# Seven-product pairs in five blocks of the up projections of a GLA and MoBA decoder trunk

## The chip, the cores and the metric

One core of one Trainium2 chip. The time is device microseconds of one execution of the whole program; lower is better. Engines: TensorE (PE; its weight loads are PEld), VectorE (DVE), ScalarE (ACT), GpSimd (POOL) and SyncE (SP, which issues the weight transfers).

## The reference

A trunk of two layers on 256 tokens with model width 2048, all in float32. Layer 0 mixes tokens with gated linear attention (GLA), layer 1 with block attention (MoBA) on a shared K and V. After each comes a gated feed-forward block, which is where most of the change lies:

```python
def conv_ffn(x, norm_w, w_up, conv_w, conv_b, w_down):
    h = rms_norm(x, norm_w) @ w_up            # 2048 x 11264
    hp = jnp.pad(h, ((0, 0), (CONV_WIDTH - 1, 0), (0, 0)))
    acc = conv_b
    for j in range(CONV_WIDTH):
        acc = acc + conv_w[j] * hp[:, j:j + S]
    a, u = jnp.split(acc, 2, axis=-1)
    return (jax.nn.silu(a) * u) @ w_down      # 5632 x 2048
```

## The kernel before

Every large matrix product is made in float32 precision from a reduced-precision matmul format: each operand is split into a high and a low part, and three products (high by high, low by high, high by low) are added in PSUM. One matmul takes 128 rows of depth, 128 tokens and 512 weight columns. Operands of the activations are made once per norm; the weights are streamed.

**The weight stream** (class WeightStream, lines 62 to 166) loads chunks of 128 x 2048 through SP into three raw buffers and splits each 1024-column half: ScalarE casts the high part `whi` (line 151), VectorE subtracts it to get `wlo` (line 153). The half's parts come from pools of three buffers each. Halves are split in a fixed order, up to two steps ahead of TensorE in the program (three in blocks with seven-product pairs). One call of step() hands one half to TensorE; jobs that were put off with after(n, job) run n steps later.

**Plain groups** (gemm_tok, line 296): 512 output columns, 8 steps of 12 matmuls, 96 in all, into two PSUM banks. High parts are line 305, the low part of the weights line 308. Each up projection has 22 such groups J.

**Blocks of pairs** (down, line 334, matmuls at line 361): 1024 output columns at once. The depth is taken in pairs k of 256 rows, so that a pair is a product of 2 x 2 matrices of blocks (two depths, two halves of the columns, two halves of the tokens). A plain pair makes the eight block products with 24 matmuls in two steps. A pair marked + in ORDERS makes seven block products of sums and differences instead, by Strassen's and Winograd's scheme: 21 matmuls in four steps. It needs sums of the weights (t13 and t24, lines 112 to 114: one VectorE operation of 1024 columns, two of 512), four halves to split instead of two (one of 512 columns, three of 1024), and sums of the activations (combine, line 314). The pairs after the bar in an order, the tail, come last and finish first the left column half (f = 0), then the right (f = 1), two steps each for two tail pairs. The seven sums p1 to p7 and p8 lie in eight PSUM banks; for names in DIRECT they are put together by one ScalarE copy and eight VectorE additions of 512 columns (lines 413 to 428). Before the change the K, MoBA query, gate, output and down projections use blocks of this kind; the up projections use only plain groups.

**After an up group**: ScalarE scales its two banks into `tok` (line 792), VectorE transposes (line 793), POOL stores the tile in DRAM (line 797) and loads it back feature-major (line 803). 7 and 9 steps after the group's end two convolutions run (convolve, line 807): two ScalarE activations (line 812), four VectorE operations of some 255 columns (lines 816, 818), a Silu, a product (line 821) and a split into the pair `hid`, VectorE's part of which is line 438. Seven of the hidden pairs (EARLY) are also combined there for the down projection.

**Memory**: a pool of 38 shared slots of 128 x 512 words or less holds operands, sums, `hid`, the weight sums and some of the split buffers; six temporary buffers hold short-lived tiles.

**Gates and start**: gated (line 745, its activations at line 627) makes the operands of the GLA output projection from transfers that POOL issues (line 527); for the last two gate heads it runs 12 and 13 steps after the head's product. At the start eight idle products of zeros keep TensorE occupied (line 223) while ScalarE's queue loads the input (line 229); the first operand `xw` is made at line 268.

Of the kernel before, what the change touches and what calls it, by code (L numbers as in the profile page):

```python
# [37 lines left out]
def _order(text):  # L38
# [13 lines left out]
    "k": [_order("0 1+ 2 3+ 4+ | 5 6 7")],  # L52
    "mq": [_order("0 1 2+ 3 4 | 5 6 7")],
    "g": [_order("0 2 5 1+ 3+ 4+ | 6 7")],
}
DIRECT = ("k", "mq", "g")

# [4 lines left out]
class WeightStream:  # L62
# [4 lines left out]
    def __init__(self, tc, raw, parts):  # L67
        self.tc, self.nc, self.raw, self.parts = tc, tc.nc, raw, parts
        self.chunks, self.halves = [], []
        self.tiles, self.split = {}, {}  # L70
        self.n_dma = self.n_split = 0
        self.cuts, self.lead, self.deep, self.free = {}, {}, set(), set()
        self.sums, self.slot, self.first = {}, None, None
        self.latest = []
# [53 lines left out]
    def prefetch(self, i):  # L128
        nc = self.nc
        while self.n_split < len(self.halves):  # L130
# [17 lines left out]
            for a, b in ((0, 512), (512, 1024)) if n < 2 else ((0, src.shape[1]),):  # L148
                with self.tc.issue_after(self.first) if n + a else nullcontext():
                    with self.in_order(n, 0):  # L150
                        one = nc.scalar.copy(hi[:, a:b], src[:, a:b])  # L151
                with self.in_order(n, 1):
                    two = nc.vector.tensor_sub(lo[:, a:b], src[:, a:b], hi[:, a:b].bitcast(F32))  # L153
                self.latest = [one.ins, two.ins]
# [15 lines left out]
def trunk(ctx: ExitStack, tc: tile.TileContext, xT, x_tok, cst, msk, w1p, w2a, w_k, w_qa, w_v2, w_v, w_gs, w_g, w_go,  # L170
          w_up0, w_dn0, w_kk, w_kv, w_mq, w_mqs, w_mo, w_up1, w_dn1, rel, onehot, out):
    nc = tc.nc
# [5 lines left out]
    parts = ctx.enter_context(tc.tile_pool(name="parts", bufs=3))  # L178
    tmp = ctx.enter_context(tc.tile_pool(name="tmp", bufs=6))
    small = ctx.enter_context(tc.tile_pool(name="small", bufs=2))  # L180
# [12 lines left out]
    def accs():  # L193
# [3 lines left out]
    plan = [(w_v2, 1, 16384), (w_v, 2, 8192), (w_k, "k", None), (w_qa, 2, 8192), (w_gs, "g", None), (w_g, 2, 8192), (w_go, "go", None),  # L197
            (w_up0, FT // 2, 8192), (w_dn0, "dn0", None),
            (w_mq, (0,), 8192), (w_mqs, "mq", None), (w_mq, (1,), 8192), (w_kk, 4, 8192), (w_kv, 4, 8192), (w_mo, "mo", None),
            (w_up1, FT // 2, 8192), (w_dn1, "dn1", None)]  # L200
    for w, groups, cols in plan:
        if cols is None:
            for g, order in enumerate(ORDERS[groups]):
                ws.add_quads(w, g, order, groups in ("go", "mo"), groups == "mo")
            continue
        for g in range(groups) if isinstance(groups, int) else groups:
            ws.add(w, g, cols)
# [13 lines left out]
    junk = bank("junk", (128, 512))  # L221
    for _ in range(8):
        T.matmul(junk, ones, idle, start=True, stop=True)
    V.memset(mhalf, -0.5)
    gn = keep.tile([128, KT], F32, name="gn")

    def load_x(p, queue=nc.sync):
        for i in range(2) if p == 0 else (slice(0, 2),):
            queue.dma_start(h[p][:, i], xT[p].rearrange("a (b c) -> a b c", b=2)[:, i])

    load_x(0, A)
    A.dma_start(gn, cst[:, C_GN:C_GN + KT])
    A.preload_act_table_set("natural_log_exp_and_others")
    load_x(1, A)

# [28 lines left out]
    def make_xw(p, c, name, src):  # L264
        x = slot([128, 2, 2 * S], F32R, name)
        for i in range(2):
            n = col(c + 2 * p + i)
            hi = A.activation(x[:, i, :S], src[:, i, :], AF.Copy, scale=n)  # L268
            ws.first = ws.first or hi.ins
            V.scalar_tensor_tensor(x[:, i, S:], src[:, i, :], n, x[:, i, :S].bitcast(F32),  # L270
                                   op0=OP.mult, op1=OP.subtract)
        return x
# [53 lines left out]
    def combine_parts(k, xs, into):  # L326
        t = temp("whole")
        V.tensor_add(t, xs[k][:, :, :S], xs[k][:, :, S:])
        combine(k, [(t[:, i, :128], t[:, i, 128:]) for i in range(2)], into)

    def sevens(name):
        return {k for order, _ in ORDERS[name] for k, seven in order if seven}

    def down(name, xs, combos, res, done, jobs):

        for b, (order, n_tail) in enumerate(ORDERS[name]):
            loaded = (name, b) != ("dn1", 1)
            new = [k for k, seven in order if seven and k not in combos]
            todo = {i: list(js) for i, js in jobs.get(b, {}).items()}
            for k in new:  # L340
                at = next(i for i, (k_, _) in enumerate(order) if k_ == k)
                todo.setdefault(max(at - 2, 0), []).append(lambda k=k: combine_parts(k, xs, combos))
            p = {}
# [96 lines left out]
    class Norm:  # L440
# [26 lines left out]

        def spread(self):

            d = temp("diag", (128, 2, 128))  # L470
            for t in range(2):
                V.tensor_scalar(d[:, t], ident, self.col[:, t:t + 1], None, op0=OP.mult)
            ps = bank("row", (128, S))
            spread_sum(ps, d.rearrange("p a b -> p (a b)"))
            self.rstd = small.tile([128, S], F32, name="rstd_h")
            A.copy(self.rstd, ps)

# [9 lines left out]
    after(17, nrm.close)  # L487
    after(18, nrm.spread)
    xs = rows(nrm.xs)
# [61 lines left out]
    nc.gpsimd.memset(smask.rearrange("p (c j) -> p c j", j=64)[:, :, 0:1], 0.0)  # L551
    zaug = slot([17, S], F32, "zaug")
    nc.gpsimd.memset(zaug, 1.0)
    la = [slot([128, 2, 2 * S], F32, f"la{i}") for i in range(2)]
# [4 lines left out]
    def gate_rank():  # L559
        zps = bank("z", (128, 512))  # L560
        for kt in range(KT):
            T.matmul(zps, w1s[kt // 8][:, kt % 8, :], xs(kt), start=kt == 0, stop=kt == KT - 1)  # L562
        zt, zl = temp("zt", (16, S)), temp("zl", (16, S))
        A.copy(zt, zps[:16, S:])
        A.copy(zl, zps[32:48, :S])
        V.tensor_add(zt, zt, zl)
        V.tensor_add(zt, zt, zps[:16, :S])
        V.tensor_mul(zaug[:16, :], zt, nrm.rstd[:16, :S])
        A.copy(zst[0:17], zaug)
        A.copy(zst[32:49], zaug)  # L570
        V.tensor_sub(zst[64:81], zaug, zst[0:17].bitcast(F32))
# [204 lines left out]
    for hd in (2, 3):  # L776
        z = gemm_tok(xs, 1, lambda ps: gate(hd, ps))
        through(hd, z, [(12 + i, lambda f, c=2 * hd + i: gated(c, f)) for i in range(2)])

    def ffn(layer, nrm, then):  # L780
# [47 lines left out]

        f = {}
        for J in range(FT // 2):  # L830
            z = gemm_tok(xs, 1, square)
            after(1, lambda J=J, z=z: store(J, z))
            after(2, lambda J=J: f.update({J: load(J)}))
            for i in range(2):
                after(7 + 2 * i, lambda J=J, i=i: convolve(2 * J + i, f[J][:, 2 * i:2 * i + 2, :]))
        then(hid, sums)
# [279 lines left out]
def _pairs(w):  # L1116
    k, n = w.shape
    return _groups(w.reshape(k, 2, n // 256, 128).transpose(0, 2, 1, 3).reshape(k, n), 512)

# [68 lines left out]
```

## Time and profile before

| | |
|---|---|
| median of 3 runs | 2168.76 us (2167.27 to 2171.57) |
| profiled execution | 2167.28 us |
| its span | 2165.5 us |
| TensorE matmuls | 9666, busy 2158.0 us (100% of the span) |
| VectorE | 1671.6 us (77%) |
| ScalarE | 1301.1 us (60%) |
| GpSimd | 291.5 us (13%) |
| DMA | 510.10 MB, 236 GB/s on average |

The profile is one execution, so a sum of durations from it is compared with 2167.28 us; the median of the runs lies 1.48 us higher. Busy times of TensorE come from modelled ends of pipelined matmuls: look at the distance between starts rather than at the share. A group of instructions in the rows has its line, engine, operation, what it writes and reads (`wlo<-wraw,whi`), shapes and count.

### The profile page before, as it was taken

To read this page: it belongs to the slowest core of one execution; us is meant where nothing else is said; L and a number is where in the kernel's file an instruction comes from. 1 tells how busy PE (TensorE), PEld (TensorE's weight loads), DVE (VectorE), ACT (ScalarE), POOL (GpSimd) and SP (SyncE) were. 2 spreads that over 40 slices of the span, in tenths; PEclk is the share of its full clock that TensorE was granted. 3 is DMA by queue.
4 is the path that set the end of the run, shared out by engine and by line. 5 is a ranking of instruction groups with operands and counts; after the bars stand their busy time and mean duration, and the time that the engine had idled before them with its cause. 6 is when DMAs were issued, how large, how long until landed. Compare 5 with 4: busy or idle time off the path is not lost.

```text
span 2165.5 us, 27041 instructions
## 1 busy us (share of the span) xinstructions
PE 2158.0 (100%) x9666; PEld 1789.5 (83%) x9666; DVE 1671.6 (77%) x2317; ACT 1301.1 (60%) x1881; POOL 291.5 (13%) x448
## 2 busy tenths in 40 slices
PE   9999999999999999999999999999999999999999
PEld 7888888888888888888888888888888888888887
DVE  6787788677777767898977787775777777779987
ACT  7656665565655656555566676565656565655554
POOL 1011111111111111000022241011111111110000
PEclk9999999999999999999999999999999999999999
DMA  8465676677777777675676887566787777775655
GB/s 321 178 232 196 214 263 241 219 234 251 236 247 237 247 237 244 212 253 211 234 262 246 269 270 240 213 234 225 236 248 235 249 235 248 237 252 214 233 199 171
DMA packets 90313, 510.10 MB, mean 236 GB/s; under 512 B 13714, under 2 KB 14754, under 8 KB 40259
## 3 DMA queue, kind: packets, MB, share of 16 engines
q1 hardware_dynamic: 60290, 417.05, 55.5%
q0 software_dynamic: 29024, 90.28, 14.6%
q8 instruction: 75, 1.23, 0.2%
q10 hardware_dynamic: 864, 1.06, 0.1%
q14 instruction: 60, 0.48, 0.1%
HBM read 463.22 MB, written 45.11 MB: 235 GB/s over the span
## 4 chain that ended last, share of the span: by engine, by line
PE 99%; DMA 1%; DVE 0%; ACT 0%; issue 0%; ACTq 0%; DVEq 0%
PE acc L305 42%; PE p L361 34%; PE acc L308 21%; PE hf L859 0%; DMA wraw<-w_go 0%; PE sT L705 0%; PE o L722 0%; PE s L972 0%; DMA h<-xT 0%; PE z L562 0%; PE o L508 0%; PE s L970 0%; DVE wlo L153 0%; PE o L507 0%; PE o L506 0%; PE o L505 0%
## 5 line engine op out<-in xcount | busy, mean ns | idle before, releaser
L153 DVE TENSOR_TENSOR wlo<-wraw,whi 128x1024 fp32r<-128x1024 f32 (+1 forms) x786 | 924.1, 1186 | 379.8 <-ACT whi L151 363.6
L151 ACT CAST whi<-wraw 128x1024 fp32r<-128x1024 f32 (+1 forms) x786 | 794.9, 1021 | 630.0 <-PE acc L305 390.6
L305 PE MATMUL acc<-whi,xw 128*128 128x512 f32 x3456 | 856.5, 390 | 1.3 <-ACT xw L268 1.3
L305 PEld LDWEIGHTS acc<-whi,xw 128*128 128x128 f32 x3456 | 648.9, 188 | 136.9 <-ACT xw L268 2.0
L308 PE MATMUL acc<-wlo,xw 128*128 128x512 f32 x1728 | 463.6, 390 | 0.0
L308 PEld LDWEIGHTS acc<-wlo,xw 128*128 128x128 f32 x1728 | 324.7, 188 | 67.4
L361 PE MATMUL p<-whi,hid 128*128 128x512 f32 x1058 | 284.4, 389 | 0.0
L361 PEld LDWEIGHTS p<-whi,hid 128*128 128x128 f32 x1058 | 198.4, 188 | 41.1
L151 ACT CAST whi<-t 128x1024 fp32r<-128x1024 f32 x100 | 102.9, 1052 | 84.6 <-PE p L361 70.4
L361 PE MATMUL p<-wlo,hid 128*128 128x512 f32 x529 | 153.1, 389 | 0.0
L803 POOL DMA_DIRECT2D upT<-turned x176 | 114.1, 655 | 147.1 <-DMA turned<-z 58.2
L153 DVE TENSOR_TENSOR wlo<-t,whi 128x1024 fp32r<-128x1024 f32 x100 | 119.9, 1221 | 15.0 <-PE p L361 8.1
L361 PE MATMUL p<-whi,comb 128*128 128x512 f32 x400 | 129.8, 389 | 0.0
L305 PE MATMUL acc<-whi,xkv 128*128 128x512 f32 x512 | 127.9, 391 | 0.0
L797 POOL DMA_DIRECT2D turned<-z x44 | 34.1, 775 | 679.1 <-DVE au L816 572.9
L361 PEld LDWEIGHTS p<-wlo,hid 128*128 128x128 f32 x529 | 99.3, 188 | 20.6
L305 PEld LDWEIGHTS acc<-whi,xkv 128*128 128x128 f32 x512 | 94.6, 188 | 18.7
L812 ACT ACTIVATE au<-upT,cs 128x256 f32<-128x256 f32 x176 | 95.8, 593 | 17.3 <-DMA upT<-turned 17.3
L361 PEld LDWEIGHTS p<-whi,comb 128*128 128x128 f32 x400 | 75.0, 188 | 15.5
L361 PE MATMUL p<-whi,xw 128*128 128x512 f32 x314 | 82.9, 389 | 0.0
L816 DVE SCALAR_TENSOR_TENSOR au<-upT,cs,au 128x255 f32<-128x255 f32 x176 | 77.0, 472 | 6.3 <-ACT au L812 6.1
L818 DVE SCALAR_TENSOR_TENSOR au<-upT,cs,au 128x254 f32<-128x254 f32 x176 | 80.5, 478 | 0.0
(241 smaller groups left out, 1897.5 us busy)
## 6 DMA issues: line engine op xcount, KB each, us to landing
wraw<-w_up SPq DMA_DIRECT2D x176, 1024.0 KB, 5.2
wraw<-w_dn SPq DMA_DIRECT2D x88, 1024.0 KB, 5.0
turned<-z POOLq DMA_DIRECT2D x44, 512.0 KB, 3.5
upT<-turned POOLq DMA_DIRECT2D x176, 128.0 KB, 4.9
wraw<-w_go SPq DMA_DIRECT2D x16, 1024.0 KB, 5.9
wraw<-w_kk SPq DMA_DIRECT2D x16, 1024.0 KB, 5.9
wraw<-w_kv SPq DMA_DIRECT2D x16, 1024.0 KB, 5.9
wraw<-w_mo SPq DMA_DIRECT2D x16, 1024.0 KB, 4.9
```

The costliest lines, as they stand in the source:

```text
L151: one = nc.scalar.copy(hi[:, a:b], src[:, a:b])
L153: two = nc.vector.tensor_sub(lo[:, a:b], src[:, a:b], hi[:, a:b].bitcast(F32))
L305: T.matmul(ps[t], xs(kt)[:, x0 + 128 * t:x0 + 128 * t + 128], hi[:, c:c + 512], start=kt == 0 and x0 == 0, stop=False)
L308: T.matmul(ps[t], xs(kt)[:, 128 * t:128 * t + 128], lo[:, c:c + 512], start=False, stop=kt == KT - 1)
L361: T.matmul(p[n], x[xi], w[wi][:, 512 * f:512 * f + 512], start=n not in begun, stop=left[n] == 0)
L797: nc.gpsimd.dma_start(turned[J].rearrange("(a i) r q c -> (i r) a (q c)", a=4), z.rearrange("p (a q) t c -> p a (q t c)", a=4))
L803: nc.gpsimd.dma_start(f[32 * q:32 * q + 32].rearrange("p a (i c) -> p (a i) c", i=4), turned[J][:, :, q, :].rearrange("a r c -> r a c"))
L812: A.activation(au[:, i, :], t[:, i, :], AF.Identity, bias=col(cb + n), scale=col(cw + 2 * 2 * FT + n))
L816: V.scalar_tensor_tensor(au[:, i, 1:], t[:, i, :S - 1], col(cw + 2 * FT + n), au[:, i, 1:], op0=OP.mult, op1=OP.add)
L818: V.scalar_tensor_tensor(au[:, i, 2:], t[:, i, :S - 2], col(cw + n), au[:, i, 2:], op0=OP.mult, op1=OP.add)
```

## The change

Ten blocks of two up groups, J = 0, 4, 8, 12 and 16 with their neighbours in each layer, go through down() with the order `0 1 2 3+ 4 5+ | 6 7`; the other twelve groups of each layer stay plain. The rows of a block reach the store two steps apart instead of eight, and the convolutions come 9 and 11 steps later (7 and 9 for the last two groups). The activation sums of pairs 3 and 5 are made once in each layer. Beside that: eleven idle products instead of eight at the start, the start's loads in a fixed order, the first operand half on VectorE, seven temporary buffers, the last gate heads 10 and 11 (first) and 11 and 12 steps later (second), a smaller tile for the norm factor, and sums of activations in the down projections made four pairs ahead and queued behind the latest split.

```diff
@@ orders @@
+    "up": [_order("0 1 2 3+ 4 5+ | 6 7")] * 5,
     "g": [_order("0 2 5 1+ 3+ 4+ | 6 7")],
-DIRECT = ("k", "mq", "g")
+DIRECT = ("k", "mq", "g", "up")
+BLOCKS = (0, 4, 8, 12, 16)
+GROUPS = [j for j in range(FT // 2) if j not in BLOCKS and j - 1 not in BLOCKS]
@@ WeightStream @@
-        self.sums, self.slot, self.first = {}, None, None
+        self.sums, self.slot, self.first = {}, None, []
...
-                with self.tc.issue_after(self.first) if n + a else nullcontext():
+                with self.tc.issue_after(self.first[min(n, 1)]) if n + a else nullcontext():
@@ trunk: pools, plan @@
-    tmp = ctx.enter_context(tc.tile_pool(name="tmp", bufs=6))
+    tmp = ctx.enter_context(tc.tile_pool(name="tmp", bufs=7))
...
-            (w_up0, FT // 2, 8192), (w_dn0, "dn0", None),
+            (w_up0s, w_up0, "up"), (w_dn0, "dn0", None),
...
+        if cols == "up":
+            for J in range(FT // 2):
+                if J in BLOCKS:
+                    ws.add_quads(w, BLOCKS.index(J), ORDERS["up"][BLOCKS.index(J)], False, False)
+                elif J in GROUPS:
+                    ws.add(groups, GROUPS.index(J), 8192)
+            continue
@@ start @@
-    for _ in range(8):
+    for _ in range(11):
         T.matmul(junk, ones, idle, start=True, stop=True)
...
-    load_x(0, A)
-    A.dma_start(gn, cst[:, C_GN:C_GN + KT])
-    A.preload_act_table_set("natural_log_exp_and_others")
-    load_x(1, A)
+    begun = load_x(0, 0, A)
+    with tc.issue_after(begun.ins):
+        begun = A.dma_start(gn, cst[:, C_GN:C_GN + KT])
+    with tc.issue_after(begun.ins):
+        begun = load_x(0, 1, A)
+    with tc.issue_after(begun.ins):
+        A.preload_act_table_set("natural_log_exp_and_others")
+        load_x(1, queue=A)
@@ make_xw @@
-            hi = A.activation(x[:, i, :S], src[:, i, :], AF.Copy, scale=n)
-            ws.first = ws.first or hi.ins
+            if not ws.first:
+                hi = V.tensor_scalar(x[:, i, :S], src[:, i, :], n, None, op0=OP.mult)
+            else:
+                hi = A.activation(x[:, i, :S], src[:, i, :], AF.Copy, scale=n)
+            ws.first.append(hi.ins)
@@ down @@
+    def combine_late(k, xs, into):
+        with ws.behind():
+            combine_parts(k, xs, into)
...
-    def down(name, xs, combos, res, done, jobs):
+    def down(name, xs, combos, res, done, jobs, only=None):
         for b, (order, n_tail) in enumerate(ORDERS[name]):
+            if only not in (None, b):
+                continue
...
-                todo.setdefault(max(at - 2, 0), []).append(lambda k=k: combine_parts(k, xs, combos))
+                back, make = {"dn": (4, combine_late), "up": (2, combine_late)}.get(name[:2], (2, combine_parts))
+                todo.setdefault(max(at - back, 0), []).append(lambda k=k, make=make: make(k, xs, combos))
@@ Norm.spread, zaug @@
-            self.rstd = small.tile([128, S], F32, name="rstd_h")
-            A.copy(self.rstd, ps)
+            A.copy(to, ps[:to.shape[0]])
...
+    zaug = slot([17, 2, S], F32, "zaug")
+    rstd, zaug = zaug[:16, 1], zaug[:, 0]
@@ last two gate heads @@
-        through(hd, z, [(12 + i, lambda f, c=2 * hd + i: gated(c, f)) for i in range(2)])
+        through(hd, z, [(8 + hd + i, lambda f, c=2 * hd + i: gated(c, f)) for i in range(2)])
@@ ffn @@
-        f = {}
+        f, first = {}, {}
+
+        def onto(J, z):
+            after(1, lambda: store(J, z))
+            after(2, lambda: f.update({J: load(J)}))
+            for i in range(2):
+                after((9 if J < FT // 2 - 2 else 7) + 2 * i, lambda i=i: convolve(2 * J + i, f[J][:, 2 * i:2 * i + 2, :]))
+
+        def up_rows(t, J, x):
+            if t == 0:
+                first[J] = slot([128, 16, 2, 32], F32, "z")
+            A.activation(x, x, AF.Copy, scale=nrm.woven[:, t:t + 1])
+            V.transpose(first[J][:, :, t, :], x.rearrange("p (a b) -> p a b", b=32))
+            if t:
+                onto(J, first[J])
+
+        x_sums = {}
         for J in range(FT // 2):
-            z = gemm_tok(xs, 1, square)
-            after(1, lambda J=J, z=z: store(J, z))
-            after(2, lambda J=J: f.update({J: load(J)}))
-            for i in range(2):
-                after(7 + 2 * i, lambda J=J, i=i: convolve(2 * J + i, f[J][:, 2 * i:2 * i + 2, :]))
+            if J in BLOCKS:
+                b = BLOCKS.index(J)
+                down("up", nrm.xs, x_sums, None, lambda t, c, x: up_rows(t, J + c - 2 * b, x), {}, b)
+            elif J in GROUPS:
+                onto(J, gemm_tok(xs, 1, square))
```

The second layer's weights are treated alike, and the host cuts each up matrix into the columns of the blocks and those of the plain groups.

## Rows read from the trace of the kernel before

**Rows 1.** The page: span, busy time of each engine, chain that ended last.

```profile
span 2165.5 us, 27041 instructions
...
PE 2158.0 (100%) x9666; PEld 1789.5 (83%) x9666; DVE 1671.6 (77%) x2317; ACT 1301.1 (60%) x1881; POOL 291.5 (13%) x448
...
PE 99%; DMA 1%; DVE 0%; ACT 0%; issue 0%; ACTq 0%; DVEq 0%
```

**Rows 2.** Stretches (us; busy us and count per engine; granted clock; DMA share; GB/s).

```profile
382.00:855.00 473.00, 473.00 (x2089) 391.75 (x2088) 339.78 (x498) 276.13 (x389) 70.69 (x105) 1.00 0.75 240
...
500.00:543.00 43.00, 43.00 (x191) 35.62 (x190) 31.86 (x50) 26.06 (x37) 6.72 (x10) 1.00 0.77 248
...
1934.00:2048.00 114.00, 114.00 (x505) 94.39 (x504) 104.89 (x131) 66.70 (x80) 5.56 (x9) 1.00 0.64 226
...
208.00:224.00 16.00, 16.00 (x72) 13.26 (x71) 15.73 (x21) 15.03 (x27) 1.07 (x1) 1.00 0.27 85
```

**Rows 3.** Chain in order of time: the last down projection (start, us, what).

```profile
1934.35 227.13 PE p L361 x1002
```

**Rows 4.** Timeline, layer 0's up projection: start, us, operation, idle before and releaser.

```profile
500.94 1.05 ACT L151 CAST whi<-wraw 128x1024 fp32r<-128x1024 f32 x1 [1.66 <-PE acc L305]
...
502.02 1.23 DVE L153 TENSOR_TENSOR wlo<-wraw,whi 128x1024 fp32r<-128x1024 f32 x1 [1.48 <-ACT whi L151]
...
503.42 1.07 PE L308 MATMUL acc<-wlo,xw 128*128 128x512 f32 x4
...
508.86 1.07 PE L308 MATMUL acc<-wlo,xw 128*128 128x512 f32 x4
```

**Rows 5.** Groups by shape: busy us, mean ns of one, idle before.

```profile
L153 DVE TENSOR_TENSOR wlo<-wraw,whi 128x1024 fp32r<-128x1024 f32 x732 | 890.4, 1223 | 374.6 <-ACT whi L151 359.1 <-PE p L361 6.2 <-PE acc L308 4.6
...
L112 DVE TENSOR_TENSOR t<-wraw 128x1024 f32<-128x1024 f32 x50 | 61.1, 1222 | 17.9 <-DMA wraw<-w_dn 9.2 <-DMA wraw<-w_go 6.0 <-DMA wraw<-w_mo 2.3
...
L821 DVE TENSOR_TENSOR au<-au 128x256 f32<-128x256 f32 x88 | 36.9, 419 | 1.2 <-ACT au L820 1.0
...
L153 DVE TENSOR_TENSOR wlo<-wraw,whi 128x512 fp32r<-128x512 f32 x54 | 37.0, 687 | 5.2 <-ACT whi L151 4.5 <-PE p L361 0.4 <-PE acc L308 0.3
...
L818 DVE SCALAR_TENSOR_TENSOR au<-upT,cs,au 128x254 f32<-128x254 f32 x176 | 80.5, 478 | 0.0
```

**Rows 6.** Timeline of VectorE in the K projection, four operations back to back.

```profile
123.69 4.62 DVE L153 TENSOR_TENSOR wlo<-wraw,whi 128x1024 fp32r<-128x1024 f32 x4
```

**Rows 7.** Timeline of the GLA output projection; last, gate transfers to landing.

```profile
299.83 2.18 POOL L527 DMA_DIRECT2D turned<-gates  x4 [2.88 <-PE p L361]
...
312.95 1.05 ACT L151 CAST whi<-wraw 128x1024 fp32r<-128x1024 f32 x1 [3.93 <-DMA wraw<-w_go]
315.86 1.07 PE L361 MATMUL p<-whi,go 128*128 128x512 f32 x4
...
317.09 0.68 DVE L438 TENSOR_TENSOR go<-g,go 128x512 fp32r<-128x512 f32 x1
...
317.83 1.20 PE L361 MATMUL p<-whi,go 128*128 128x512 f32 x4 [0.90 <-DVE go L438]
...
turned<-gates POOLq DMA_DIRECT2D x4, 128.0 KB, 7.0
```

**Rows 8.** Timeline of the start; last, its slow stretch as in rows 2.

```profile
1.32 3.78 PE L223 MATMUL junk<-idle,ones 128*128 128x512 f32 x8 [1.32 <-POOL idle L220]
...
5.13 0.69 DVE L153 TENSOR_TENSOR wlo<-wraw,whi 128x512 fp32r<-128x512 f32 x1 [4.11 <-ACT whi L151]
...
5.82 0.51 ACT L268 ACTIVATE xw<-h,gn 128x256 fp32r<-128x256 f32 x1 [0.72 <-DMA h<-xT]
...
6.38 2.07 PE L305 MATMUL acc<-whi,xw 128*128 128x512 f32 x4 [1.29 <-ACT xw L268]
...
10.31 0.62 PE L308 MATMUL acc<-wlo,xw 128*128 128x512 f32 x2
...
6.30:9.60 3.30, 3.22 (x8) 2.54 (x9) 2.83 (x5) 2.51 (x6) 0.00 (x0) 1.00 1.01 402
```

More of the change, by code (lines that the diff above doesn't have):

```diff
@@ L170, in trunk @@
 def trunk(ctx: ExitStack, tc: tile.TileContext, xT, x_tok, cst, msk, w1p, w2a, w_k, w_qa, w_v2, w_v, w_gs, w_g, w_go,
-          w_up0, w_dn0, w_kk, w_kv, w_mq, w_mqs, w_mo, w_up1, w_dn1, rel, onehot, out):
+          w_up0s, w_up0, w_dn0, w_kk, w_kv, w_mq, w_mqs, w_mo,
+          w_up1s, w_up1, w_dn1, rel, onehot, out):
     nc = tc.nc
@@ L197, in trunk @@
     plan = [(w_v2, 1, 16384), (w_v, 2, 8192), (w_k, "k", None), (w_qa, 2, 8192), (w_gs, "g", None), (w_g, 2, 8192), (w_go, "go", None),
-            (w_up0, FT // 2, 8192), (w_dn0, "dn0", None),
+            (w_up0s, w_up0, "up"), (w_dn0, "dn0", None),
             (w_mq, (0,), 8192), (w_mqs, "mq", None), (w_mq, (1,), 8192), (w_kk, 4, 8192), (w_kv, 4, 8192), (w_mo, "mo", None),
-            (w_up1, FT // 2, 8192), (w_dn1, "dn1", None)]
+            (w_up1s, w_up1, "up"), (w_dn1, "dn1", None)]
     for w, groups, cols in plan:
+        if cols == "up":
[5 more added lines that the diff above has]
+            continue
         if cols is None:
@@ L225, in trunk, with load_x @@
     gn = keep.tile([128, KT], F32, name="gn")
-    def load_x(p, queue=nc.sync):
-        for i in range(2) if p == 0 else (slice(0, 2),):
-            queue.dma_start(h[p][:, i], xT[p].rearrange("a (b c) -> a b c", b=2)[:, i])
-    load_x(0, A)
-    A.dma_start(gn, cst[:, C_GN:C_GN + KT])
-    A.preload_act_table_set("natural_log_exp_and_others")
-    load_x(1, A)
+    def load_x(p, i=slice(0, 2), queue=nc.sync):
+        return queue.dma_start(h[p][:, i], xT[p].rearrange("a (b c) -> a b c", b=2)[:, i])
+    begun = load_x(0, 0, A)
[6 more added lines that the diff above has]
+        load_x(1, queue=A)
     ws.cuts = {0: ((0, 512), (512, 1024), (1024, 2048)), 1: ((0, 1024), (1024, 2048))}
@@ L466, in weave, with spread @@
                     A.copy(self.woven[32 * i:32 * i + 32, t:t + 1], self.col[32 * q:32 * q + 32, i // 2:i // 2 + 1])
-        def spread(self):
+        def spread(self, to):
             d = temp("diag", (128, 2, 128))
@@ L487, in trunk @@
     after(17, nrm.close)
-    after(18, nrm.spread)
+    zaug = slot([17, 2, S], F32, "zaug")
+    nc.gpsimd.memset(zaug[:, 0], 1.0)
+    rstd, zaug = zaug[:16, 1], zaug[:, 0]
+    after(18, lambda: nrm.spread(rstd))
     xs = rows(nrm.xs)
@@ L551, in trunk @@
     nc.gpsimd.memset(smask.rearrange("p (c j) -> p c j", j=64)[:, :, 0:1], 0.0)
-    zaug = slot([17, S], F32, "zaug")
-    nc.gpsimd.memset(zaug, 1.0)
     la = [slot([128, 2, 2 * S], F32, f"la{i}") for i in range(2)]
@@ L567, in gate_rank @@
         V.tensor_add(zt, zt, zps[:16, :S])
-        V.tensor_mul(zaug[:16, :], zt, nrm.rstd[:16, :S])
+        V.tensor_mul(zaug[:16, :], zt, rstd)
         A.copy(zst[0:17], zaug)
@@ L1117, in _pairs, with _columns @@
     k, n = w.shape
-    return _groups(w.reshape(k, 2, n // 256, 128).transpose(0, 2, 1, 3).reshape(k, n), 512)
+    return w.reshape(k, 2, n // 256, 128).transpose(0, 2, 1, 3).reshape(k, n)
+def _columns(w, starts, width):
+    import numpy as np
+    w = _pairs(w)
+    return np.concatenate([w[:, 512 * j:512 * j + width] for j in starts], axis=1)
 def _buckets():
@@ L1166 @@
         "w_go": _quads(a["gla_w_out"][0], ORDERS["go"]),
-        "w_up0": _pairs(a["ffn_w_up"][0]),
+        "w_up0s": _quads(_columns(a["ffn_w_up"][0], BLOCKS, 1024), ORDERS["up"]),
+        "w_up0": _groups(_columns(a["ffn_w_up"][0], GROUPS, 512), 512),
         "w_dn0": _quads(a["ffn_w_down"][0], ORDERS["dn0"]),
@@ L1173 @@
         "w_mo": _quads(a["moba_w_out"][0], ORDERS["mo"]),
-        "w_up1": _pairs(a["ffn_w_up"][1]),
+        "w_up1s": _quads(_columns(a["ffn_w_up"][1], BLOCKS, 1024), ORDERS["up"]),
+        "w_up1": _groups(_columns(a["ffn_w_up"][1], GROUPS, 512), 512),
         "w_dn1": _quads(a["ffn_w_down"][1], ORDERS["dn1"]),
```

## The prediction

> **What bounds the kernel now.** I read the page first, for the shares; then the table of stretches, to see where TensorE has room; then the timeline and the groups by shape, for prices. On the page TensorE is busy for 2158.0 of 2165.5 us and VectorE for 77% [rows 1]. A busy TensorE could still be a slow one, so look at the distance between matmuls: from one step's lo products at 503.42 to those two steps later at 508.86 lie 24 matmuls in 5.44 us, 0.2267 us each [rows 4]. In the last down projection the chain of waits runs through 1002 of them in 227.13 us, again 0.2267 [rows 3], although its pairs alternate between eight and seven products. So the distance is the same with a light and with a heavy load on VectorE, and TensorE is never held: in layer 0's up projection it is busy for 473.00 of 473.00 us [rows 2]. A matmul left out there is worth 0.2267 us as long as nothing else becomes late.
>
> **The change, part by part.**
>
> 1. Products left out. A block of two groups had 192 matmuls. With two seven-product pairs of eight it has 6 x 24 + 2 x 21 = 186. Ten blocks (five in each layer) lose 60 matmuls: 60 x 0.2267 = **13.60 us**, all on the path.
>
> 2. What VectorE gets for it. A plain pair has two splits of 1024 columns, 1.223 us each; a seven-product pair has three of those and one of 512 columns (0.687), so 4.36 instead of 2.45, +1.91. The weight sums add one operation of 1024 columns and two of 512: 1.222 + 2 x 0.687 = 2.60 [rows 5]. Two pairs: 2 x 4.51 = 9.0 us. Putting the eight sums together takes eight additions of 512 columns, 8 x 0.687 = 5.5. Together 14.5 us more for each block. ScalarE gets two casts per seven-product pair and a copy per block and is at 60% [rows 1]; that I cost at nothing.
>  Is there room? Four groups (a block and two plain ones) will take 186 x 0.2267 + 43.5 = 85.7 us of TensorE. Today VectorE has 31.86 us in 43 [rows 2], 63.5 in 85.7; with 14.5 more it is 78.0, or 91%. The down projection of layer 1 runs at 104.89 of 114 us, 92%, and the gate projection at 15.73 of 16, both with TensorE busy throughout [rows 2]. So the mean load is one this kernel already carries.
>  Within a block it is tighter. Its own work is 12 x 1.223 + 2 x (4.36 + 2.60) + 5.5 + 4 x 0.687 for the transposes = 36.9 us, and four convolutions come due in it (two of each group before), each 4 x 0.478 + 2 x 0.419 = 2.75 [rows 5]: 47.9 us against TensorE's 42.16. Durations overstate it, though: four splits back to back take 4.62 us, so they start 1.13 apart, 0.09 less than one lasts [rows 6]. For 62 operations that is 5.6 us, and 42.3 remain: just what TensorE needs. What absorbs bunching is the lead. A cast starts at 500.94, when TensorE gives a buffer back; its difference is ready at 502.02 + 1.23 = 503.25 and is used from 508.86 [rows 4]: VectorE may fall 5.6 us behind before TensorE waits. The seven-product pairs (4.76 us of TensorE, 7.0 of VectorE) overdraw this by 2.2 each, a plain pair between them gives back 5.44 - 2.45 = 3.0, less a convolution of 2.75. That stays inside the lead.
>  The wait that may be left is bounded below by 0 (TensorE has no idle time here to win) and above by 5.6 us a block, the whole excess by durations. I take 0.1 us a block, **+1.0 us** in all, near the lower end, because both loaded stretches in rows 2 run without a wait.
>
> 3. Activations of the up projection. Two pair sums are combined in each layer, with the first block alone. The up rows now come in pairs, two steps apart, with convolution lags of 9 rather than 7. POOL stores and loads two groups in a row; in the steady stage it has 6.72 us of work in 43 [rows 2], and nine steps (24.5 us at 2.72) cover two transfers. Weight bytes and the number of weight transfers on SP stay the same. Cost nothing; if the lag were too short, a convolution would wait on ScalarE and hold the casts queued behind it.
>
> 4. Gates one step earlier. The GLA output projection has one gap: four matmuls from 315.86 would end their turn at 316.77, the next starts at 317.83, after the last operand's lo part (317.09 + 0.68) [rows 7]. 1.06 us are lost. That gate was queued behind a cast that sat 3.93 us for its weights until 312.95. One step (2.72 us) earlier it stands ahead of this cast. The transfers it needs are issued from 299.83 to 302.01 and land 7.0 us later, about 309, while the cast behind it has no weights before 312.95 anyway: a late landing would be covered. Ends: -1.06 and 0; I take **-1.06**.
>
> 5. The start. The first product begins at 6.38, right after ScalarE made its operand (5.82 + 0.51). Ten matmuls then begin until 10.31: 3.93 us in place of 2.27, so 1.66 lost [rows 8]. [...] The operand moves to VectorE, at worst behind the split of 5.13 to 5.82 and then not slower than ScalarE's 0.51, so at 6.33 as now. [...] I take **-1.0**, as what precedes the slow stretch is the pause that goes.
>  [...]
>
> 6. A smaller norm tile, a seventh temporary buffer and later combinations in the down projections: nothing, since no wait in those stages names them.
>
> Sum: -13.60 + 1.0 - 1.06 - 1.0 = **-14.7 us**. The profiled execution took 2167.28 us (span 2165.5 and 1.8 around it), so 2152.6 by its own time. The median of the runs is 1.48 higher, which gives 2154.1; I say **2154**.
>
> **The rivals.**
>
> A. *VectorE sets the pace of the blocks* (slower). For it: 47.9 us of durations against 42.16. Against it: 15.73 of 16 us in the gate projection without a wait, and operations that overlap. If the excess came out in full, ten blocks would lose 57 us: 2168.8 - 15.7 + 57 = 2210. It decides from 1.57 us lost per block (15.7 / 10). Chance 0.08.
>  [...] The 98% stretch of rows 2 shows that the share alone costs nothing.
>
> B. *Short waits inside the seven-product stretches.* For it: convolutions due at steps 9 and 11 of a block fall between its two seven-product pairs, so the lead is spent twice. Against it: the down projections do the like. With 0.3 to 1.2 us a block, 3 to 12 us go back: 2156 to 2165, middle 2161. Chance 0.13.
>
> C. *Buffers run out late in each layer.* The kernel has 38 shared slots. In the fifth block eight operands, seven early combinations, two new ones, up to sixteen hidden pairs, two weight sums, a pair of split buffers and an up tile make 38, so a split may wait for a release. One step (2.72 us) in both layers: 2154 + 5.4 = 2159.5. For it: the count. Against it: nothing waits for a slot now, and the lead covers it. Chance 0.07.
>
> D. *Nothing is left of it*, the gaps and the start staying and a wait of 1.4 us in each block: about 2168. Chance 0.04.
>
> **How the numbers follow.** The forecast has 0.68 with its own range 2151 to 2157: below by the start's full -1.66 on the profiled time (2167.28 - 16.3), above by the start and the gate gap giving nothing. A measurement of this kernel tells about 0.2%, 4.3 us, from no change, so faster means under 2164.4. Faster: 0.68 + 0.11 of B + 0.07 of C = 0.86. Same: 0.02 of B, 0.03 of D and 0.01 of A = 0.06. Slower: 0.07 of A and 0.01 of D = 0.08. The range runs from 2150.5 to 2163, which takes in the forecast, C and two thirds of B.
>
> **What would show it.** In the changed profile: 60 matmuls fewer and three idle ones more; the same 0.2267 us between matmuls in the blocks; layer 0's up projection about 6.8 us shorter; VectorE near 91% there; no gap before the products that start at 317.83 now; and a first product near 6.4 that is followed sooner by short distances. The prediction is wrong if TensorE waits for splits inside the blocks: gaps behind the wlo tile, several in each block, over 1 us together.

## The result, and the profile after

The changed kernel is slower: median 2192.47 us of six runs (2182.28 to 2198.68), against 2167.07 us of six runs of the kernel before (2166.35 to 2171.57). The ratio is 1.0103, with a 95% interval of [1.0085, 1.012]. The forecast was 2154 us and faster, with 2163 as the upper end, so both the sign and the range were wrong. The profiled execution took 2192.77 us, 25.5 more than that of before.

The page of the changed kernel, its shares of busy time (the same lines as in [rows 1]):

```profile
span 2191.0 us, 27236 instructions
...
PE 2159.1 (99%) x9609; PEld 1782.7 (81%) x9609; DVE 1795.7 (82%) x2522; ACT 1337.9 (61%) x1934; POOL 291.6 (13%) x448
```

The matmuls came out as planned: 9666 - 60 + 3 idle ones = 9609. Yet TensorE, busy all the time before, now has gaps. To find the stage, I compared the first matmul of each stage in both traces:

| stage | before, us | after, us | difference |
|---|---|---|---|
| up to layer 0's up projection | 375.56 | 374.04 | -1.52 |
| layer 0's up projection | 479.65 | 493.75 | +14.10 |
| layer 0's down projection | 229.67 | 231.05 | +1.38 |
| MoBA | 369.66 | 369.66 | 0 |
| layer 1's up projection | 479.64 | 490.65 | +11.01 |
| layer 1's down projection | 231.32 | 231.84 | +0.52 |

The loss is in the two up projections. Each has 30 matmuls fewer, so each should be 30 x 0.2267 = 6.80 us shorter. What delays TensorE there costs 14.10 + 6.80 = 20.9 and 11.01 + 6.80 = 17.8, together **38.7 us**.

What TensorE waits for, over the whole run (us in total, times, longest), the line that holds nearly all of it:

```profile
PE p L385 <- ACT whi L154: 26.0, 13, 3.8
```

In the kernel before, the same list names one wait behind the first product:

```profile
PE p L361 <- DVE go L438: 0.9, 1, 0.9
```

The changed kernel waits for ScalarE's cast of a weight half, the high part, not for VectorE's low part, which is what the prediction had watched. By the distances between matmuls, the two layers' waits over 0.6 us sum to 26.2 us, one or two in each of eight blocks (3.89, 3.91, 3.88, 2.69 us in layer 0, 3.92, 1.64, 4.36, 1.90 in layer 1); 9.7 us more are lost on the matmuls just behind five of them, most of which start 0.427 instead of 0.2267 us apart, and 2.8 us are small gaps. The first block of each layer, in which no convolution falls due, loses nothing.

One such wait in the timeline of ScalarE (start, duration, engine, line, operation; in brackets the idle time before it and what ended it):

```profile
483.26 2.08 ACT L836 ACTIVATE au<-upT,cs 128x256 f32<-128x256 f32 x4
485.24 1.04 ACT L154 CAST whi<-t 128x1024 fp32r<-128x1024 f32 x1
488.74 0.42 ACT L844 ACTIVATE au<-au 128x256 f32<-128x256 f32 x1 [2.46 <-DVE au L842]
490.66 0.42 ACT L844 ACTIVATE au<-au 128x256 f32<-128x256 f32 x1 [1.50 <-DVE au L842]
491.33 0.74 ACT L461 CAST hid<-au 128x256 fp32r<-128x256 f32 x2 [0.25 <-DVE au L845]
491.98 0.58 ACT L439 COPY c<-p 128x512 f32<-128x512 f32 x1
493.14 0.62 ACT L461 CAST comb<-comb 128x512 fp32r<-128x512 f32 x1 [0.59 <-DVE comb L338]
493.67 1.04 ACT L154 CAST whi<-t 128x1024 fp32r<-128x1024 f32 x1
```

and of VectorE and TensorE beside it:

```profile
477.02 1.23 DVE L115 TENSOR_TENSOR t<-wraw 128x1024 f32<-128x1024 f32 x1 [2.50 <-DMA wraw<-w_up0s]
...
483.12 0.69 DVE L117 TENSOR_TENSOR t<-wraw,t 128x512 f32<-128x512 f32 x1
...
494.74 1.23 DVE L156 TENSOR_TENSOR wlo<-t,whi 128x1024 fp32r<-128x1024 f32 x1 [0.25 <-ACT whi L154]
...
494.76 0.79 PE L385 MATMUL p<-whi,comb 128*128 128x512 f32 x1 [3.73 <-ACT whi L154]
```

The cast at 493.67 makes the high part of t24, the second weight sum of pair 5. Its input was complete at 483.12 + 0.69 = 483.81. It starts 9.9 us later, and ScalarE isn't busy all of that time: it stands idle for 2.46 + 1.50 + 0.25 + 0.59 = 4.8 us. In these rows ScalarE starts its instructions in the order of the program, and ahead of this cast stand the rest of the two convolutions due at steps 9 and 11 (two Silus, two casts of hidden pairs, the cast of an early combination) and a copy of the block's own. Each Silu waits for VectorE's filter taps (L842), each hidden cast for VectorE's product (L845), the combination for VectorE's sums (L338). So the cast goes back and forth between two engines with them, although it needs none of them.

### The profile page after: what moved, and what is told of

It reads as the page before. It is cut to its first block, busy times and chain, and to the rows that moved or that the text cites. A ratio compares the mean times of both kernels' runs of the same rounds, so it can differ in the third digit from the quotient of the medians.

```text
span 2191.0 us, 27236 instructions
## 1 busy us (share of the span) xinstructions
PE 2159.1 (99%) x9609; PEld 1782.7 (81%) x9609; DVE 1795.7 (82%) x2522; ACT 1337.9 (61%) x1934; POOL 291.6 (13%) x448
## 3 DMA queue, kind: packets, MB, share of 16 engines
q10 hardware_dynamic: 864, 1.06, 0.1%
## 5 line engine op out<-in xcount | busy, mean ns | idle before, releaser
L322 PE MATMUL acc<-whi,xw 128*128 128x512 f32 x2176 | 539.9, 390 | 0.1
L322 PEld LDWEIGHTS acc<-whi,xw 128*128 128x128 f32 x2176 | 407.6, 188 | 86.0 <-ACT whi L154 1.4
L385 PE MATMUL p<-whi,xw 128*128 128x512 f32 x1394 | 371.2, 395 | 0.0
L385 PEld LDWEIGHTS p<-whi,xw 128*128 128x128 f32 x1394 | 265.9, 191 | 56.2 <-ACT whi L154 1.0
L325 PE MATMUL acc<-wlo,xw 128*128 128x512 f32 x1088 | 290.9, 389 | 0.0
L325 PEld LDWEIGHTS acc<-wlo,xw 128*128 128x128 f32 x1088 | 204.2, 188 | 42.6
L385 PE MATMUL p<-whi,comb 128*128 128x512 f32 x560 | 185.9, 395 | 26.1 <-ACT whi L154 26.0
L385 PE MATMUL p<-wlo,xw 128*128 128x512 f32 x697 | 196.6, 390 | 0.0
L385 PEld LDWEIGHTS p<-wlo,xw 128*128 128x128 f32 x697 | 131.5, 189 | 27.6
L115 DVE TENSOR_TENSOR t<-wraw 128x1024 f32<-128x1024 f32 x70 | 85.4, 1220 | 38.6 <-DMA wraw<-w_dn 11.7
```

The source lines that it names most:

```text
L115: V.tensor_sub(t13, src[:, 512:1536], src[:, 0:1024])
L322: T.matmul(ps[t], xs(kt)[:, x0 + 128 * t:x0 + 128 * t + 128], hi[:, c:c + 512], start=kt == 0 and x0 == 0, stop=False)
L325: T.matmul(ps[t], xs(kt)[:, 128 * t:128 * t + 128], lo[:, c:c + 512], start=False, stop=kt == KT - 1)
L385: T.matmul(p[n], x[xi], w[wi][:, 512 * f:512 * f + 512], start=n not in begun, stop=left[n] == 0)
```

## The experiments

Three explanations were to be told apart; the expectations use these letters or describe them:

- **Q**, the queue: the cast of t24 stands behind the convolutions in ScalarE's order. Move the convolutions behind the block, or the cast ahead of them, and the waits go.
- **L**, load: VectorE's work in that place is too much, whatever ScalarE's order. This is the prediction's rival A or B.
- **D**, the detour on VectorE: the first weight sum of pair 5 waits 2.50 us for its weights at 477.02, and the second sum of pair 3 stands queued behind it.

All ratios are to the kernel before, timed beside it.

**1. The convolutions of the group before a block run 17 steps later, behind the block's last sum.**

```diff
-  after((9 if J < FT // 2 - 2 else 7) + 2 * i, …
+  after((17 if J + 1 in BLOCKS else 9 if J < FT // 2 - 2 else 7) + 2 * i, …
```

> The convolutions of the group before a block move from steps 9 and 11 of the block (between and inside its two seven-product pairs) to steps 17 and 19 (its tail); nothing else differs from the changed kernel. [...] Theory L (VectorE has too much work in a block, whatever its order): the waits move to the tail or the next group, and the time stays over 2175. Theory D (VectorE's own wait of 2.5 to 3.2 us for the weights of pair 5 uses up the lead): about half of the waits stay, 2165 to 2178.

Measured: 2159.32 us, 0.9943 [0.9924, 0.9961]. What TensorE waits for:

```profile
PE p L385 <- ACT whi L154: 3.2, 8, 1.0
```

One number in the code turns the loss into a gain: 26.0 us of waits become 3.2, and no stretch of slow matmuls is left (the granted clock of the profiled execution is 1.000, where it was 0.995). Q had expected under 4 us of waits and 2150 to 2158 us; the time lies 1.3 us over that. The arithmetic is the same. That speaks for Q; but it also moves VectorE's part of the convolutions, so L isn't yet out.

**2. A lag of 7 for all groups, as before the change.**

```diff
-  after((9 if J < FT // 2 - 2 else 7) + 2 * i, …
+  after(7 + 2 * i, …
```

> All convolutions 7 and 9 steps after their group, as before the change, so those of the group before a block come at its steps 7 and 9 instead of 9 and 11. Theory Q: in ScalarE's order the cast of pair 5's second weight sum still has one Silu, one hidden cast and the combination cast ahead of it, half of the chain, so waits of 1 to 3 us a block stay: 2165 to 2188 us. Theory L: as the changed kernel, 2185 to 2195. Theory D: as the changed kernel too.

Measured: 2259.27 us, 1.0421 [1.0375, 1.0468], far beyond what was expected. The waits of TensorE:

```profile
PE p L385 <- ACT whi L154: 56.5, 21, 7.3
```

and, of ScalarE's waits, those of the filters for their rows:

```profile
ACT au L836 <- DMA upT<-turned: 118.7, 39, 10.8
```

A second way to the same wait shows here: the rows come back from DRAM after the convolution has reached the head of ScalarE's queue, and the casts behind it stand still while it waits, up to 10.8 us. In the kernel before these waits sum to 17.3 us (20 of them, the longest 2.1), and TensorE's lead covered them. So the change needed a lag longer than 7; the one it took put the convolutions ahead of the wrong cast.

**3. No blocks in the up projections, all other edits kept.**

```diff
-BLOCKS = (0, 4, 8, 12, 16)
+BLOCKS = ()
 ...
```

> Everything of the change but the blocks: all 22 groups of each up projection are plain, with lag 9, and the start, the gates, the seventh temporary buffer and the late sums are as changed. All theories: no wait in the up projections; the start gives 1.1 us and the gates 0.4 net, so 1 to 2 us less than before, 2165 to 2166.5. If the lag of 9 or the late sums cost something by themselves, it is over 2168.

Measured: 2169.72 us, 0.999 [0.9972, 1.0008]: no difference. The side edits do a part of their work (the start gives 1.0 us in this trace) and lose it again: a gap of 1.15 us between matmuls stands in the GLA output projection, and layer 0's down projection takes 2.5 us longer than before, 1.18 of them in one gap. Without the blocks there is no loss.

**4. One seven-product pair in each block instead of two.**

```diff
-    "up": [_order("0 1 2 3+ 4 5+ | 6 7")] * 5,
+    "up": [_order("0 1 2 3+ 4 5 | 6 7")] * 5,
```

> The changed kernel with one seven-product pair per block instead of two (order 0 1 2 3+ 4 5 | 6 7): 30 matmuls more than the changed kernel, 30 fewer than before. The convolutions stay at steps 9 and 11, after the casts of the only such pair. Theory Q: no wait over 1 us in a block, since no weight sum's cast stands behind a convolution; 30 x 0.2267 = 6.8 us and 1.5 from the side edits less than before: 2159 to 2164 us. Theory L: VectorE has 4.5 us less in a block than in the changed kernel but still bunches; some waits, 2168 to 2180.

Measured: 2162.07 us, 0.9966 [0.9955, 0.9978]. The stretch of layer 0's up projection (us, then busy time of PE, PEld, DVE, ACT, POOL with counts, granted clock, DMA share, GB/s):

```profile
382.00:848.00 466.00, 466.00 (x2057) 385.85 (x2057) 376.26 (x562) 288.22 (x407) 70.67 (x105) 1.00 0.74 242
```

The lag is 9, the convolutions are where they were, and TensorE has no wait: there is no t24 of pair 5 behind them. Half of the products saved bring their time. VectorE has less to do in these blocks too, so this run alone doesn't part Q from L.

**5. The order of the weight sums on VectorE.** Each pair's first sum is queued behind the last sum of the pair before, and so no longer holds it.

```diff
-        V.tensor_sub(t13, src[:, 512:1536], src[:, 0:1024])
+        with self.tc.issue_after(self.summed) if self.summed else nullcontext():
+            V.tensor_sub(t13, src[:, 512:1536], src[:, 0:1024])
 ...
-        V.tensor_sub(t24[:, 512:], src[:, 1536:], t24[:, :512])
+        self.summed = V.tensor_sub(t24[:, 512:], src[:, 1536:], t24[:, :512]).ins
```

> The changed kernel, with the first weight sum of a pair queued on VectorE behind the last weight sum of the pair before, so that VectorE's wait for pair 5's weights no longer stands ahead of pair 3's second sum. Theory D: the waits shrink by half or more, 2160 to 2178 us. Theory Q: the small gaps ahead of pair 3's second sum (0.13 to 1.06 us) go, those of 2 to 4 us ahead of pair 5's stay: 2182 to 2192. Theory L: no difference, 2185 to 2195.

Measured: 2197.68 us, 1.012 [1.0085, 1.0155]. Waits of TensorE:

```profile
PE p L386 <- ACT whi L155: 26.7, 10, 3.8
```

The small gaps ahead of pair 3's sum are gone or under 0.1 us, the large ones ahead of pair 5's are all there, and the time lies over every range expected. D isn't the main cause.

**6. VectorE's load put back without ScalarE's.** Experiment 1, plus seven unused additions of 256 columns at steps 9 and 11 of each block but the first, which stand for VectorE's part of the two convolutions in about its time and place; ScalarE gets nothing.

```diff
+        def load_vector():
+            idle_ = temp("idle_sum", (128, S))
+            with ws.behind():
+                for _ in range(7):
+                    last = V.tensor_add(idle_, cs[:, :S], cs[:, S:2 * S])
+            ws.latest = [ws.latest[0], last.ins]
 ...
+                for s in (9, 11) if J else ():
+                    after(s, load_vector)
```

> The kernel with the convolutions in the tail of the block (2159.32 us), plus work for VectorE alone: at steps 9 and 11 of every block but the first of each layer, seven additions of 256 columns whose result nobody uses, placed ahead of the differences of pair 5's weight sums, so that VectorE does there about what the two convolutions gave it (14 operations at 0.33 to 0.42 us, 4.6 to 5.9 us a block), while ScalarE has nothing extra. Theory Q (it is the chain that goes from ScalarE to VectorE and back ahead of the cast that costs the time): little comes back, 0 to 1.5 us a block, 2159 to 2171 us. Theory L (VectorE's work at this place is what counts): 2 to 4 us a block as in the changed kernel, 2176 to 2195 us.

Measured: 2175.27 us, 1.0026 [1.0011, 1.004], 16 us more than experiment 1. ScalarE, VectorE and TensorE around one such place:

```profile
484.36 2.00 ACT L154 CAST whi<-t 128x1024 fp32r<-128x1024 f32 x2 [1.19 <-PE p L385]
...
484.66 3.18 DVE L873 TENSOR_TENSOR idle_sum<-cs 128x256 f32<-128x256 f32 x7
...
489.49 3.18 DVE L873 TENSOR_TENSOR idle_sum<-cs 128x256 f32<-128x256 f32 x7
...
492.59 2.35 DVE L156 TENSOR_TENSOR wlo<-t,whi 128x1024 fp32r<-128x1024 f32 x2
...
493.86 0.73 PE L385 MATMUL p<-wlo,comb 128*128 128x512 f32 x2 [1.15 <-DVE wlo L156]
```

This lies between the theories. ScalarE casts both weight sums of pair 5 at 484.36, in time; VectorE is held up ahead of their differences until 492.59, and TensorE waits 1.15 us for it, where it waited 3.73 for the cast in the changed kernel. So work put in at that place of VectorE's order does cost, without any chain on ScalarE. But it is 16 us and not 33 (2192.47 - 2159.32) by the medians, and in the up projections of the profiled traces 11.2 and not 34.3, without slow matmuls (this trace is of an execution of 2171.14 us). The additions are queued in one piece at either step, unlike the convolutions, so the run shows the size of VectorE's share roughly and doesn't measure it.

**7. The convolution in three stages, each queued behind the latest cast.** The lag stays 9; the Silu and product run one step after the filters, the hidden cast another step later.

```diff
-            A.activation(au[:, 0, :], au[:, 0, :], AF.Silu)
+            after(1, lambda: activate(j, au))
+
+        def activate(j, au):
+            with ws.behind():
+                A.activation(au[:, 0, :], au[:, 0, :], AF.Silu)
 ...
+            after(1, lambda: hidden(j, au))
+
+        def hidden(j, au):
 ...
-            split(hid[-1][:, j % 2, :S], hid[-1][:, j % 2, S:], au[:, 0, :])
+            with ws.behind():
+                split(hid[-1][:, j % 2, :S], hid[-1][:, j % 2, S:], au[:, 0, :])
```

> The changed kernel with each convolution in three steps (filters, then one step later the Silu and product, then the split), each queued behind the latest cast; lags stay at 9 and 11. In ScalarE's order the cast of pair 5's second weight sum then stands behind two Silus and one hidden cast, no longer behind the copy, the second hidden cast and the combination cast. Theory Q: the waits shrink but stay, 0.5 to 3 us a block: 2160 to 2180 us. Theory L: as the changed kernel, 2182 to 2198.

Measured: 2168.43 us, 0.9996 [0.9982, 1.001]. TensorE's waits:

```profile
PE p L385 <- ACT whi L154: 11.5, 10, 1.8
```

and ScalarE's timeline ahead of the cast of t24:

```profile
489.41 0.42 ACT L848 ACTIVATE au<-au 128x256 f32<-128x256 f32 x1 [3.94 <-DVE au L842]
491.33 0.42 ACT L848 ACTIVATE au<-au 128x256 f32<-128x256 f32 x1 [1.50 <-DVE au L842]
492.00 0.41 ACT L461 CAST hid<-au 128x256 fp32r<-128x256 f32 x1 [0.25 <-DVE au L849]
492.31 1.04 ACT L154 CAST whi<-t 128x1024 fp32r<-128x1024 f32 x1
```

The amount of work on VectorE and the lag of the filters are what they were; the ends of the convolutions come later, on VectorE too, and 24 us (2192.47 - 2168.43) are gone. Both Silus still stand ahead of the cast and wait 3.94 and 1.50 us for VectorE; the second hidden cast, the copy and the combination have moved behind it. So the cast comes 1.4 us earlier (492.31 against 493.67), not ten. No matmul here starts at the slow distance (the granted clock of the profiled execution is 1.000).

**8. All repairs together.** Lag 17 (experiment 1), the order of the sums (experiment 5), the combinations of the down projections as before, and the gates' lag taken back for one head.

```diff
-                back, make = {"dn": (4, combine_late), "up": (2, combine_late)}.get(name[:2], (2, combine_parts))
+                back, make = {"up": (2, combine_late)}.get(name[:2], (2, combine_parts))
 ...
-        through(hd, z, [(8 + hd + i, …
+        through(hd, z, [((12 if hd == 2 else 11) + i, …
```

> Meant to beat both: convolutions of the group before a block in its tail, weight sums of a pair behind those of the pair before, sums of activations in the down projections as before the change (two pairs ahead, not queued behind the split), and the gate heads 12 and 13 (first) and 11 and 12 (second) steps later. Theory Q: the 0.3 to 0.7 us gaps ahead of pair 3's second sum, the one of 1.2 us in layer 0's down projection and those near 297 us go; 2150 to 2156 us. Theory D: as well. Theory L: no better than with the convolutions moved alone, 2157 to 2160.

Measured: 2153.36 us (2152.63 to 2155.07), 0.9928 [0.9912, 0.9944], 15.4 us less than the kernel before and faster than both. Two stretches of its trace, layer 0's up projection and one block in it with the groups beside it:

```profile
382.00:848.00 466.00, 466.00 (x2057) 385.87 (x2056) 398.30 (x597) 297.36 (x424) 70.70 (x105) 1.00 0.74 242
...
462.00:505.00 43.00, 43.00 (x191) 35.59 (x191) 40.43 (x57) 28.22 (x39) 3.37 (x5) 1.00 0.73 242
```

No wait is left in any block, and each up projection takes 472.85 us, 6.80 less than before, to the hundredth what 30 matmuls are worth. VectorE is busy for 40.43 of 43 us, 94%, with TensorE never held. Outside the blocks this trace still has waits: a gap of 1.09 us in the GLA output projection, and layer 1's down projection takes 233.52 us, 2.2 more than before.

**9. Experiment 8 with the lag of 9 put back.**

```diff
-  after((17 if J + 1 in BLOCKS else 9 if J < FT // 2 - 2 else 7) + 2 * i, …
+  after((9 if J < FT // 2 - 2 else 7) + 2 * i, …
```

> The fastest version so far (2153.36 us) with one thing put back: the convolutions of the group before a block 9 and 11 steps after it, as in the changed kernel. It differs from that version in the lag alone. [...] If the other three edits of that version were what helped, it stays under 2165.

Measured: 2194.97 us, 1.0122 [1.0102, 1.0141], where Q and L had both expected 2178 to 2198 us; TensorE's waits:

```profile
PE p L386 <- ACT whi L155: 20.7, 8, 3.8
```

The lag alone is worth 2194.97 - 2153.36 = 41.6 us, about what the up projections lose in the changed kernel (38.7).

**10. Experiment 8 with a lag of 13 instead of 17.** VectorE's part of the convolutions stays inside the block, only behind the cast of t24.

```diff
-  after((17 if J + 1 in BLOCKS else …
+  after((13 if J + 1 in BLOCKS else …
```

> The fastest version with those convolutions 13 and 15 steps after their group: in ScalarE's order the first of them then stands just behind the cast of pair 5's last weight sum, while VectorE still gets them within the last seven-product pair. Theory Q: it is enough that the cast stands ahead; no wait over 1 us in a block, 2152 to 2158 us. Theory L: VectorE is as crowded there as with lag 9 to 11, 1 to 2 us a block: 2162 to 2172.

Measured: 2154.05 us, 0.9929 [0.9914, 0.9944]. ScalarE's timeline in the same block:

```profile
485.28 2.00 ACT L155 CAST whi<-t 128x1024 fp32r<-128x1024 f32 x2 [2.42 <-DVE wlo L157]
487.19 1.09 ACT L837 ACTIVATE au<-upT,cs 128x256 f32<-128x256 f32 x2
```

Four steps are enough. Both casts of weight sums now stand ahead of the first filter and run at 485.28, and TensorE waits for no split in any block (a plain group between two of them waits 0.7 us); the filters, Silus and products follow in the same block with all their VectorE work. The job's place decides, and L, the amount of VectorE's work in a block, falls as the cause. The later lag also moves that work behind the difference of t24 in VectorE's order, so this run doesn't part the two engines' orders; experiment 6 does, and VectorE's gives the smaller share there.

## Why the prediction was wrong, by its own steps

The failing step was **step 3**. It gave the new lag a price of nothing, because the transfers have time enough, and named only one danger, a lag too *short*, by which a convolution holds the casts behind it. Experiment 2 shows that danger to be real (56.5 us of waits). But a lag of 9 puts two convolutions just ahead of the cast of t24, and the same holding comes from their round trips to VectorE instead of from DMA. The step never asked which cast stands next behind the convolutions on ScalarE. **Step 2** helped it: ScalarE "at 60%" was taken as free. ScalarE is at 61% after, and has 4.8 us of idle time ahead of the very cast that TensorE waits for.

The term that came out wrong is step 2's wait: +1.0 us forecast, 38.7 measured. That is 4.8 for each of the eight later blocks on average, and 1.8 to 7.5 by block: five of the eight lie over the upper bound of 5.6 that the step gave, since that bound was worked out from VectorE's durations alone. I took a value near the lower end since the loaded stretches of [rows 2] ran without waits. Those rows showed that VectorE can be full; they said nothing on who stands behind whom on ScalarE.

- Step 1, right: 60 matmuls fewer at 0.2267 us, 6.80 us per layer in experiment 8.
- Step 2, VectorE's load: right that its amount fits. Experiment 8 carries it without a wait in any block, though the durations of a block exceed TensorE's time. For a lag of 9 its price was too low for VectorE alone: experiment 6 costs 1.4 us a block in its trace (11.2 over eight blocks), where the step took 0.1. Its list of a block's work also leaves out the early combinations, whose cast is one of those ahead of t24. VectorE's busy share alone set no limit here: the trace of experiment 8 shows 94% in a stretch without a wait.
- Step 4, half right. The gap of 1.06 us [rows 7] is gone, but small gaps, 0.78 us together, come back a little earlier, behind a wait of VectorE for weights. In the timeline of VectorE and TensorE:

```profile
292.82 1.23 DVE L115 TENSOR_TENSOR t<-wraw 128x1024 f32<-128x1024 f32 x1 [0.63 <-DMA wraw<-w_go]
...
297.76 0.50 PE L385 MATMUL p<-wlo,comb 128*128 128x512 f32 x1 [0.28 <-DVE wlo L156]
```

- Step 5, right: -1.0 forecast, -1.09 measured. No row of before shows that the pause ahead of the first product makes the slow stretch, and the -1.0 rests on that alone; it was my estimate, and the traces showed 1.09 in its place. Eleven idle products reach up to the first product, and most of what followed at half rate in [rows 8], 0.427 us apart, starts some 0.23 us apart (four in 1.33 us). All eleven traces with the new start reach the forty-first product 0.88 to 1.20 us earlier than the trace of before. TensorE's timeline at the start:

```profile
1.31 5.06 PE L234 MATMUL junk<-idle,ones 128*128 128x512 f32 x11 [1.31 <-POOL idle L231]
6.25 1.33 PE L322 MATMUL acc<-whi,xw 128*128 128x512 f32 x4
```

- Step 6, wrong by 1.38 + 0.52 = 1.9 us. Layer 0's down projection pays for the combinations that were moved, again by ScalarE's order; ScalarE's timeline in layer 0's down projection:

```profile
1058.94 0.62 ACT L461 CAST comb<-comb 128x512 fp32r<-128x512 f32 x1 [3.52 <-DVE comb L338]
1059.47 1.04 ACT L154 CAST whi<-t 128x1024 fp32r<-128x1024 f32 x1
```

 The cast of a combination waits 3.52 us for VectorE, and the cast of a weight sum stands behind it. With the combinations put back as they were (experiment 8) layer 0's down projection takes 229.67 us again, and 231.60 in experiment 1, which leaves them moved. In layer 1 putting them back wins nothing (233.52 us in experiment 8, 231.84 in the changed kernel, 231.32 before), and what costs time there stays open.

Of the rivals, **B** had the place, the convolutions due at steps 9 and 11 between the two seven-product pairs, but a price of 0.3 to 1.2 us a block instead of 4.8, because it counted VectorE's time alone; for that alone it was close (1.4 in experiment 6). **A** had nearer the time (2210 against 2192), by a mechanism that experiments 8 and 10 exclude. Nothing showed **C**. With the lag alone mended (experiment 1) 2159.32 is measured, 10.6 less than the kernel before beside it: inside the forecast's range, 5 us over its value. Experiments 8 and 10 come to 2153.36 and 2154.05, with the weight sums reordered and parts of steps 4 and 6 undone. That this is so near 2154 is partly luck: the blocks give their 13.6 us in full and the start its 1.0, but the gate term gives nothing in the trace of experiment 8, and layer 1's down projection loses 2.2 us.

Why 9.7 us more than the waits themselves were lost is told below. What stays open is how much of the loss VectorE's work alone makes at that place with lag 9: the additions of experiment 6 cost 16 us of the 33 that the lag gave, and in experiment 10, behind the cast and the difference, the real work costs nothing in the blocks. No run leaves the convolutions where they were in VectorE's order and puts ScalarE's cast ahead of them.

## What to carry to other kernels

Before a job is moved, write down what it passes and what it then stands ahead of on every engine (here a cast with its input ready stood 9.9 us behind such a job), and ask of each instruction that TensorE needs soon whether a chain of round trips between two engines stands ahead of it; an engine's busy share says nothing on that (61% for ScalarE here, with 26.0 us of waits for its casts). When a lag is changed, look for the next cast on the path and put the job behind it: four steps more (13 instead of 9) were worth 41 us here. A summed load that fits, even VectorE's 94% in experiment 8, is no reason to expect waits, and a low one, as ScalarE's 61%, no reason to exclude them.

## What the runs showed of the hardware that was not expected

A wait cost more than its own length. Behind the wait that ends at 494.76, TensorE starts its matmuls at about half its rate. Two stretches of the changed kernel, the wait and what follows (columns as in experiment 4), and the matmuls:

```profile
490.00:494.70 4.70, 1.03 (x5) 0.53 (x3) 3.80 (x12) 3.20 (x7) 0.00 (x0) 1.00 0.37 143
494.80:498.30 3.50, 3.50 (x9) 2.78 (x10) 3.44 (x3) 3.50 (x4) 0.00 (x0) 0.53 0.00 0
```

```profile
495.35 0.63 PE L385 MATMUL p<-whi,xw 128*128 128x512 f32 x1
495.78 0.63 PE L385 MATMUL p<-whi,comb 128*128 128x512 f32 x1
```

The granted clock is 0.53, and matmuls start 0.43 us apart instead of 0.2267. Eight to fourteen matmuls, most of them so far apart, follow each of the five waits of 3.6 to 3.9 us and lose 1.7 to 2.9 us each time, 9.7 us together; none of the waits of 1.6 to 1.9 us in this trace is followed by such a stretch (granted clock 1.00 behind them). The length of the wait alone doesn't decide it, though: in experiment 5 a wait of 3.71 us was followed by none, at a granted clock of 1.00, and one of 1.95 us by eight, at 0.64. The same dependence may be a part of why the changed kernel scatters over 16 us (2182.28 to 2198.68, at granted clocks of 0.994 to 0.997) and experiment 10 over 0.4 (all at 1.000). That was not tried apart, and it can't be all: the kernel before, at a granted clock of 0.999 to 1.000, scattered over 15 us in the runs beside experiment 1 (2166.47 to 2181.74).
